# Latent attention of a hybrid layer: value products in pairs, scores a tile ahead, and a new pace for the row gathers

## The chip, the cores and the metric

One core of a Trainium2 chip runs the whole program in one launch. The metric is the device time of one execution in microseconds; a run's figure is that of the core.

Five engines work side by side, each on its own stream of instructions: TensorE (PE in the profile; its weight loads are PEld), VectorE (DVE), ScalarE (ACT), GpSimd (POOL) and SyncE (SP). Sixteen DMA engines move data between the chip's memory and the core. A scheduler sets the order of each engine's stream when the program is built; on the chip the streams keep that order and wait for each other through semaphores.

## The reference

One layer of a diffusion backbone over 256 context tokens and 1024 latent tokens of 1024 values. Each token passes modulation by a condition vector, a norm and one input projection, which feeds windowed attention and a recurrent mixer; their outputs go through one output projection; then each token looks up experts (PEER) in two tables of 16384 rows. Cut to the part that matters here:

```
def latent_attention(q, k, v, sink, *, cos, sin, k_ctx, v_ctx):      # 8 query heads, 2 key/value heads of 64
    ...
    s_band = jnp.einsum('bnqkgd,bnckd->bkgnqc', qb, k_band).astype(jnp.float32) * ATTN_SCALE   # 3 blocks of 128 keys
    s_ctx = jnp.einsum('bnqkgd,bckd->bkgnqc', qb, k_ctx).astype(jnp.float32) * ATTN_SCALE      # 256 context keys
    s_band = jnp.where(mask, s_band, -jnp.inf)                                                 # |q - k| <= 128
    p = jax.nn.softmax(jnp.concatenate([s_band, s_ctx, sk], axis=-1), axis=-1)                 # sk: the head's sink logit
    o = (jnp.einsum('bkgnqc,bnckd->bnqkgd', p_band, v_band)
         + jnp.einsum('bkgnqc,bckd->bnqkgd', p_ctx, v_ctx))

def peer(h, w_query, sub_keys, u_tab, v_tab):
    ...
        u = jnp.take(u_tab, eid, axis=0)                                # 8 heads x 16 rows of u a token
        act = jax.nn.gelu(jnp.einsum('td,thkd->thk', xb, u))
        vv = jnp.take(v_tab, eid, axis=0)                               # and of v
        return jnp.einsum('thk,thkd->td', (g * act).astype(vv.dtype), vv)
```

## The kernel before

**Stages.** The program runs modulation, projections, recurrence, attention, output projection and ranking for the context (to about 360 us), then projection and recurrence for the latent tokens (to 541), the latent attention (541 to 792), the output projection of the latent tokens (to 905), the ranking of experts (to about 1215), the lookups that turn the ranking into gates ("spread") with the experts' first groups ("early"; to about 1814), and the expert stage proper ("dense", to 3620). Its end is the last residuals and norms.

**Experts in two ways.** Six of the eight latent token tiles compute all 16384 experts densely on TensorE: `u` (a product of the tokens with the table's rows), a gelu, a product with the gates (`a*gt`, line 763), a split in a high and a low part (line 137) and a product with `v`, added up in `rot` (lines 743, 744) and `res`. Two context tiles and the other two latent tiles fetch their own rows instead: `mix` (line 827) issues for each of 4 tiles 128 row gathers of `u` and 128 of `v` on GpSimd (lines 838, 852), 512 KB each, and VectorE takes one product over 128x1024 for each (lines 841, 858). These 1024 gathers stand in a queue. `tick(us)` (line 112) takes as many from it as the given time holds steps: 1.9 us a step as a rule (`F_STEP`), 4.0 in "ret", 1.0 in "early", 2.2 in the expert stage (`D_STEP`). So `tick` is not a time on the chip; it places the gathers among the other instructions. What is left in the queue is issued at the end.

**Latent attention.** `attend` (line 387) handles one tile of 128 queries after another, and in it one of two head groups `g` (4 query heads that share one key head) after the other. Keys are split into a high part `kh` and a low part `kl` in a reduced float format: 8 copies on ScalarE (line 402) and 4 subtractions on VectorE (line 403) ahead of all scores. The tile's queries are split in the same way (lines 412, 413) and stacked, high on 64 rows and low on the other 64. For each head four score products go into two accumulators of one `s` tile: 256 context columns and up to 384 window columns, each once with the stacked queries on 128 rows against `kh` (line 431) and once with the 64 rows of the high queries against `kl` (line 432); two products with a mask close the head (line 435). VectorE takes the maximum (line 438) and the shift (439), ScalarE the exponential with its sum (440). After the four heads, their probabilities are divided by the sum: by the string NORM, two heads on ScalarE (448), one on GpSimd and one on VectorE (450). Then for each block `j` of 128 keys, 4 transposes (455), one copy by ScalarE to `pT` (457) and one product with the values, 64 columns of the array wide (462), accumulate into 64 of the 128 rows of `po`; ScalarE copies the result over the queries (463). A tile in the middle has 5 blocks, one at an end 4. Each group ends with `tick(13)`.

A few rows of memory are shared: `kh`, `kl` and the split queries lie in tiles that later hold the normed activations (`hha`, `hla`). `finish` (the output projection) opens its weight pool before the attention.

**What sets the order.** All of this is written in program order, with buffers rotating (`bufs`), and the scheduler moves instructions ahead within an engine where buffers allow it, as the order below shows for scores among value products.

## Time and profile before

| | us |
|---|---|
| median of 3 runs (lowest to highest) | 3672.97 (3672.86 to 3684.63) |
| the profiled execution | 3664.41 |
| its span | 3662.5 |
| busy: TensorE, VectorE | 3302.0, 3111.3 |
| busy: GpSimd, ScalarE | 1705.7, 1462.7 |
| mean granted TensorE clock | 0.957 of full |

The span runs from the first to the last instruction of one profiled execution; the execution's time is measured around it. A busy share over the whole span mixes stages that have different limits, so the rows below are read by stage. In a group, "idle before" is the time in which the engine stood still just before these instructions, and behind the arrow is what ended it. The end of a TensorE instruction is modelled, and its instructions overlap in the pipeline; how long it needs for one is read from the distance of starts.

### The profile page before, as it was taken

To read this page: it belongs to the slowest core of one execution; us is meant where nothing else is said; L and a number is where in the kernel's file an instruction comes from. 1 tells how busy PE (TensorE), PEld (TensorE's weight loads), DVE (VectorE), ACT (ScalarE), POOL (GpSimd) and SP (SyncE) were. 2 spreads that over 40 slices of the span, in tenths; PEclk is the share of its full clock that TensorE was granted. 3 is DMA by queue.
4 is the path that set the end of the run, shared out by engine and by line. 5 is a ranking of instruction groups with operands and counts; after the bars stand their busy time and mean duration, and the time that the engine had idled before them with its cause. 6 is when DMAs were issued, how large, how long until landed. Compare 5 with 4: busy or idle time off the path is not lost.

```text
span 3662.5 us, 48593 instructions
## 1 busy us (share of the span) xinstructions
PE 3302.0 (90%) x16982; PEld 2718.4 (74%) x16982; DVE 3111.3 (85%) x6710; ACT 1462.7 (40%) x2272; POOL 1705.7 (47%) x1162
## 2 busy tenths in 40 slices
PE   7888879888699978888699999999999999999995
PEld 4477644434598967777688888888888888888885
DVE  4549886767799999998678898899999999899988
ACT  5743645533312334433233333333434333333333
POOL 0012454556631233246435565566556655555652
PEclk9799988999899999999799999999999999999998
DMA  8342654468851257789878898899888899888884
GB/s 330 114 155 84 210 201 133 150 213 288 303 157 39 90 180 217 233 260 308 288 243 298 300 318 299 307 331 329 314 311 309 313 329 323 320 309 308 318 319 178
DMA packets 349143, 918.20 MB, mean 251 GB/s; under 512 B 29145, under 2 KB 150105, under 8 KB 345825
## 3 DMA queue, kind: packets, MB, share of 16 engines
q0 software_dynamic: 147456, 536.94, 42.6%
q1 hardware_dynamic: 201440, 378.16, 30.1%
q8 instruction: 133, 2.18, 0.2%
q14 instruction: 114, 0.93, 0.1%
HBM read 834.48 MB, written 80.50 MB: 250 GB/s over the span
## 4 chain that ended last, share of the span: by engine, by line
PE 39%; DVE 20%; DMA 7%; issue 4%; POOL 1%; ACT 1%; SPq 0%; POOLq 0%; DVEq 0%; ACTq 0%
PE u L142 6%; PE u L140 6%; PE u L141 6%; PE rot L140 4%; PE rot L142 4%; PE rot L141 4%; DMA a<-ad 3%; DVE row L841 3%; DVE acc L858 3%; PE res L140 3%; PE res L142 3%; PE res L141 3%; DMA ad<-a 2%; DVE acc L744 2%; DVE oh L678 1%
## 5 line engine op out<-in xcount | busy, mean ns | idle before, releaser
L838 POOL DMA_INDIRECT row<-in_peer_u,eid x512 | 713.1, 1393 | 646.4 <-DVE row L841 240.5
L852 POOL DMA_INDIRECT row<-in_peer_v,eid x512 | 702.7, 1372 | 636.4 <-DVE acc L858 354.8
L140 PE MATMUL u<-hh,uh 128*128 128x384 f32 x2048 | 705.1, 344 | 40.3 <-ACT a L1009 38.2
L142 PE MATMUL u<-hh,ul 128*128 128x384 f32 x2048 | 705.4, 345 | 12.0 <-POOL ul L137 12.0
L141 PE MATMUL u<-hl,uh 128*128 128x384 f32 x2048 | 703.8, 344 | 0.0
L858 DVE SCALAR_TENSOR_TENSOR acc<-row,w,acc 128x1024 f32<-128x1024 f32 x508 | 664.7, 1308 | 28.4 <-DMA row<-in_peer_v,eid 27.1
L841 DVE SCALAR_TENSOR_TENSOR row<-row,h 128x1024 f32<-128x1024 f32 x512 | 631.1, 1246 | 60.1 <-DMA row<-in_peer_u,eid 60.0
L743 ACT ACTIVATE q<-rot 128x512 f32<-128x512 f32 x504 | 300.1, 596 | 495.1 <-PE rot L142 296.0
L140 PE MATMUL rot<-vh,ah 128*128 128x512 f32 x1024 | 408.4, 399 | 23.1 <-ACT q L743 22.5
L140 PEld LDWEIGHTS u<-hh,uh 128*128 128x128 f32 x2048 | 392.1, 191 | 48.4 <-ACT a L1009 42.0
L142 PEld LDWEIGHTS u<-hh,ul 128*128 128x128 f32 x2048 | 392.3, 192 | 15.5 <-POOL ul L137 12.9
L141 PE MATMUL rot<-vl,ah 128*128 128x512 f32 x1024 | 400.9, 392 | 0.0
L142 PE MATMUL rot<-vh,al 128*128 128x512 f32 x1024 | 400.4, 392 | 0.0
L141 PEld LDWEIGHTS u<-hl,uh 128*128 128x128 f32 x2048 | 392.5, 192 | 5.7 <-issue 2.0
L744 DVE TENSOR_TENSOR acc<-q,acc 128x512 f32<-128x512 f32 x504 | 340.7, 686 | 60.6 <-ACT q L743 57.6
L140 PE MATMUL mm<-hh,wh 128*128 128x256 f32 (+2 forms) x848 | 287.5, 339 | 11.8 <-ACT wh L136 11.8
L142 PE MATMUL mm<-hh,wl 128*128 128x256 f32 (+2 forms) x848 | 289.5, 342 | 6.2 <-POOL wl L137 3.6
L141 PE MATMUL mm<-hl,wh 128*128 128x256 f32 (+2 forms) x848 | 284.8, 336 | 0.0
L136 ACT ACTIVATE uh<-u 128x1024 fp32r<-128x1024 f32 x128 | 135.8, 1061 | 359.9 <-PE u L141 295.7
L140 PEld LDWEIGHTS rot<-vh,ah 128*128 128x128 f32 x1024 | 193.5, 189 | 82.7 <-ACT q L743 43.9
L137 POOL TENSOR_TENSOR ul<-u,uh 128x1024 fp32r<-128x1024 f32 x44 | 132.0, 2999 | 231.5 <-ACT uh L136 214.7
L142 PEld LDWEIGHTS rot<-vh,al 128*128 128x128 f32 x1024 | 193.3, 189 | 41.4
(266 smaller groups left out, 6030.8 us busy)
## 6 DMA issues: line engine op xcount, KB each, us to landing
u<-in_ut SPq DMA_DIRECT2D x128, 512.0 KB
v<-in_peer_v SPq DMA_DIRECT2D x128, 512.0 KB
gd<-stg SPq DMA_DIRECT2D x12, 4096.0 KB
gt<-gd SPq DMA_DIRECT2D x64, 768.0 KB
w<-in_w_mod SPq DMA_DIRECT2D x24, 1024.0 KB
ad<-a SPq DMA_DIRECT2D x88, 192.0 KB
a<-ad SPq DMA_DIRECT2D x44, 384.0 KB
w<-in_w_query SPq DMA_DIRECT2D x32, 512.0 KB
```

Source lines behind the costliest of these rows:

```text
L136: A.activation(hi, src, AF.Copy)
L137: return (eng or V).tensor_tensor(lo, src, hi, op=OP.subtract)
L140: T.matmul(out, lhs[0], rhs[0], start=first, stop=False)
L141: T.matmul(out, lhs[0], rhs[1], start=False, stop=False)
L142: T.matmul(out, lhs[1], rhs[0], start=False, stop=last)
L678: V.tensor_tensor(oh.rearrange(four, j=2), o2.rearrange(four, j=2), pairs(gh, ts), op=OP.mult)
L743: A.activation(q, p, AF.Copy)
L744: tick(share / (2 * (N_DENSE - N_RES)), V.tensor_tensor(y, q, y, op=OP.add))
L838: G.indirect_dma_start(out=u, out_offset=None, in_=i["peer_u"], in_offset=bass.IndirectOffsetOnAxis(ap=eid[:, k:k + 1], axis=0))
L841: V.scalar_tensor_tensor(u, u, 1.0, h2, op0=OP.mult, op1=OP.mult, accum_out=act[:, j:j + 1])
L852: G.indirect_dma_start(out=v, out_offset=None, in_=i["peer_v"], in_offset=bass.IndirectOffsetOnAxis(ap=eid[:, k:k + 1], axis=0))
L858: V.scalar_tensor_tensor(acc, v, w[:, j:j + 1], acc, op0=OP.mult, op1=OP.add)
```

## The change

1. Keys: both parts are now 128 rows high, the low part copied to the other 64 rows too, so that the score products with `kl` take the same stacked queries as those with `kh`. The keys are split in four pieces (context, columns 0 to 256, 256 to 512, 512 to 1024): 24 copies and 8 subtractions. All of them still stand before the first score product in the order.
2. Values: `scores(t, g)` of a tile come before `values` of the tile before it. For each block, both head groups' transposes and copies are followed by two products that use the two halves of the array's columns, one issued right behind the other, into the two halves of one `po`. There are 38 such pairs; ScalarE evicts 128x512 once for a tile (8) in place of 64x512 twice (16). Buffers: `pr` 4 instead of 2, `pT` 4 instead of 3.
3. Normalisation of the latent heads: all on VectorE (64 instructions; before 16 on VectorE, 16 on GpSimd, 32 on ScalarE).
4. Gathers: `tick(0.6)` for each head and `tick(1.3)` for each block replace `tick(13)` for each group, 88 us of steps instead of 208; `D_STEP` is 2.05 instead of 2.2. The count stays 1024.
5. Pools: the attention has its own key tiles, `hha` and `hla` are made after it, and the weights of `finish` lie on the other side of the memory. Its first loads keep their place in SyncE's order.

```
@@ -51,15 +51,13 @@
-D_STEP = 2.2
+D_STEP = 2.05
...
-NORM = "AAGV"
@@ -384,84 +382,109 @@
-    def attend(cond, st, ps, tiles, qT, kT, vv, spare=None):
+    def attend(cond, st, ps, tiles, qT, kT, vv):
...
-            for src, ks in ((kc, slice(0, base)), (kT, slice(base, base + S))):
+            kh, kl = (st.tile([P, 2, S + base], F32R, name=f"k{n}") for n in "hl")
+            for src, b0, k0, k1 in ((kc, 0, 0, base), (kT, base, 0, 256), (kT, base, 256, 512), (kT, base, 512, S)):
+                ks, cols = slice(b0 + k0, b0 + k1), slice(k0, k1)
                 for g in range(2):
-                    for r in range(2):
-                        A.activation(kh[half[r], g, ks], src[half[g]], AF.Copy)
-                    V.tensor_tensor(kl[half[g], ks], src[half[g]], kh[half[g], g, ks], op=OP.subtract)
-        for t in tiles:
+                    A.activation(kh[half[g], g, ks], src[half[g], cols], AF.Copy)
+                    V.tensor_tensor(kl[half[g], g, ks], src[half[g], cols], kh[half[g], g, ks], op=OP.subtract)
+                    A.activation(kh[half[1 - g], g, ks], src[half[g], cols], AF.Copy)
+                    A.activation(kl[half[1 - g], g, ks], kl[half[g], g, ks].bitcast(F32), AF.Copy)
+
+        qsp = {}
+
+        def scores(t, g):
...
+            if lat and g == 0:
+                qs = qsp[t] = st.tile([P, 2, 4, P], F32R, name="qs", bufs=2)
...
+            pr = st.tile([P, 4, W], F32, name="pr", bufs=4)
...
-                            T.matmul(out, qs[gs, g, c], kl[gs, k:k + w], start=False, stop=(bank == 0), skip_group_check=True)
+                        T.matmul(out, qh, kl[:, g, k:k + w], start=False, stop=(bank == 0), skip_group_check=True)
...
+                tick(0.6)
...
+            for c in range(4):
+                if lat:
+                    V.tensor_scalar(pr[:, c], pr[:, c], den[:, c:c + 1], None, op0=OP.mult)
+                else:
+                    A.activation(pr[:, c], pr[:, c], AF.Copy, scale=den[:, c:c + 1])
+            return pr
...
-                    T.matmul(po[gs], vb, pT, start=(j == 0), stop=(j == nk - 1))
-                A.activation(qT[gs, :, ts], po[gs], AF.Copy)
-                tick(13)
+        def values(t, prs, js):
...
+            for j in range(nk)[js]:
+                if j == 0:
+                    outs[t] = ps.tile([P, 4, P], F32, name="po")
+                po = outs[t]
+                pTs = []
+                for pr in prs:
                     pt = ps.tile([P, 4, P], F32, name="pt")
                     for c in range(4):
                         T.transpose(pt[:, c], pr[:, c, j * P:(j + 1) * P], ident)
-                    pT = st.tile([P, 4, P], F32, name="pT", bufs=3)
+                    pT = st.tile([P, 4, P], F32, name="pT", bufs=4)
                     A.activation(pT, pt, AF.Copy)
...
+                vb = vc[:, j] if lat and j < 2 else vv[:, lo + j - (2 if lat else 0)]
+                ins = T.matmul(po[half[1]], vb[:, half[1]], pTs[1], start=(j == 0), stop=(j == nk - 1))
+                with tc.issue_after(ins.ins):
+                    T.matmul(po[half[0]], vb[:, half[0]], pTs[0], start=(j == 0), stop=(j == nk - 1))
+                tick(1.3)
+                if j == nk - 1:
+                    A.activation(qT[:, :, ts], po, AF.Copy)
+
+        ahead = None
+        for t in tiles:
+            now = []
+            for g in range(2):
+                now.append(scores(t, g))
+                if ahead:
+                    values(*ahead, slice(g * 3, g * 3 + 3))
+            ahead = t, now
+        values(*ahead, slice(0, None))
@@ -930,58 +951,56 @@
...
-                attend(1, pool(es, "lat"), pool(es, "lps", space=PSUM), range(N_LAT), qT, kT, vv, (hha, hla))
...
+        fin = finish(fs, 1, range(N_LAT), qT, gy, lambda t: dest(t))
+        next(fin)
+        next(fin)
+        phase("lattend")
+        with ExitStack() as es:
+            attend(1, pool(es, "lat"), pool(es, "lps", space=PSUM), range(N_LAT), qT, kT, vv)
+        side[0] = "right"
+        hx = pool(ctx, "hx")
```

TensorE in the middle of the latent attention before (`s`: scores, `po`: values' accumulator, `pt`: transposed probabilities, `hh`, `hl` hold keys and queries):

```order
L462 MATMUL po<-pT,vv 64x512
L455 MATMUL pt<-ident,pr 128x128 x4
L462 MATMUL po<-pT,vv 64x512
L455 MATMUL pt<-ident,pr 128x128 x4
L431 MATMUL s<-hh,hl 128x256
L432 MATMUL s<-hl 128x256
L431 MATMUL s<-hh,hl 128x384
L432 MATMUL s<-hl 128x384
```

The same place now (`kh`, `kl`: keys, `qs`: queries; lines 431 and 432 are the scores, 467 the transposes, 472 and 474 the products with the values):

```order
L472 MATMUL po<-pT,vv 64x512
L474 MATMUL po<-pT,vv 64x512
L467 MATMUL pt<-ident,pr 128x128 x8
L431 MATMUL s<-kh,qs 128x256
L432 MATMUL s<-kl,qs 128x256
L431 MATMUL s<-kh,qs 128x384
L432 MATMUL s<-kl,qs 128x384
L472 MATMUL po<-pT,vv 64x512
L474 MATMUL po<-pT,vv 64x512
```

A value product stood alone, with four transposes behind it; now two stand together, eight transposes stand in a row, and scores of the next tile lie between a block's transposes and its products.

GpSimd shortly before the expert stage, before (`ul` is the low part of the experts' `u`, lines 852 and 838 are row gathers, `eid` the row numbers of one token tile):

```order
L838 DMA row<-in_peer_u,eid_2301 128x1024 x5
L137 TENSOR_TENSOR ul<-u,uh 128x1024
L838 DMA row<-in_peer_u,eid_2301 128x1024 x8
L137 TENSOR_TENSOR ul<-u,uh 128x1024
L852 DMA row<-in_peer_v,eid_2301 128x1024 x5
L137 TENSOR_TENSOR ul<-u,uh 128x1024
L852 DMA row<-in_peer_v,eid_2301 128x1024 x5
L137 TENSOR_TENSOR ul<-u,uh 128x1024
L852 DMA row<-in_peer_v,eid_2301 128x1024
```

And now (line 135 is the split, 873 and 859 the gathers):

```order
L135 TENSOR_TENSOR ul<-u,uh 128x1024
L873 DMA row<-in_peer_v,eid_2156 128x1024
L135 TENSOR_TENSOR ul<-u,uh 128x1024
L873 DMA row<-in_peer_v,eid_2156 128x1024
L135 TENSOR_TENSOR ul<-u,uh 128x1024
L873 DMA row_16254<-in_peer_v,eid_2156 128x1024
L873 DMA row_16266<-in_peer_v,eid_2156 128x1024
L873 DMA row_16515<-in_peer_v,eid_2156 128x1024
L135 TENSOR_TENSOR ul<-u,uh 128x1024 x6
L859 DMA row<-in_peer_u,eid_2297 128x1024 x3
```

Between the last splits ahead of the expert stage stood groups of gathers; now the last six splits follow each other, and the gathers come in the expert stage.

VectorE at the end of the program before, from the last additions on (`acc_16445` to `acc_16448` are the dense tiles' sums, line 858 the products of gathered rows, 816 and 817 the residuals):

```order
L744 TENSOR_TENSOR acc_16445<-q,acc_16445 128x512
L858 SCALAR_TENSOR_TENSOR acc<-row_31868,w,acc 128x1024
L744 TENSOR_TENSOR acc_16445<-q,acc_16445 128x512
L816 TENSOR_TENSOR acc<-acc,row_31873 128x1024
L744 TENSOR_TENSOR acc_16446<-q,acc_16446 128x512
L817 TENSOR_TENSOR h_31609<-acc,h_31609 128x1024
L744 TENSOR_TENSOR acc_16446<-q,acc_16446 128x512
L744 TENSOR_TENSOR acc_16447<-q,acc_16447 128x512
L147 TENSOR_SCALAR rs_m<-ss 128x1
```

And now (line 765 is the addition, 879 the product of a gathered row, 837 and 838 the residuals):

```order
L765 TENSOR_TENSOR acc_16237<-q,acc_16237 128x512
L879 SCALAR_TENSOR_TENSOR acc<-row_31893,w,acc 128x1024
L765 TENSOR_TENSOR acc_16238<-q,acc_16238 128x512
L879 SCALAR_TENSOR_TENSOR acc<-row,w,acc 128x1024
L765 TENSOR_TENSOR acc_16238<-q,acc_16238 128x512
L879 SCALAR_TENSOR_TENSOR acc<-row,w,acc 128x1024
L837 TENSOR_TENSOR row<-row,vh 128x1024
L879 SCALAR_TENSOR_TENSOR acc<-row,w,acc 128x1024
L838 TENSOR_TENSOR gt<-row,gt 128x1024
L879 SCALAR_TENSOR_TENSOR acc<-row,w,acc 128x1024
L837 TENSOR_TENSOR row<-row,vh 128x1024
L879 SCALAR_TENSOR_TENSOR acc<-row_31948,w,acc 128x1024
```

Products of gathered rows, which ended among the first additions, now stand behind all of them and among the first residuals.

## Rows read from the trace of the kernel before

**Rows 1.** By stretch: start:end, its length, busy time and instructions of each engine, PEclk, DMA, GB/s.

```profile
541.00:566.00 25.00, 22.54 (x55) 12.89 (x56) 16.58 (x33) 13.81 (x29) 5.42 (x4) 0.50 0.43 150
596.00:626.00 30.00, 27.66 (x110) 12.88 (x109) 21.14 (x40) 18.96 (x39) 15.40 (x10) 1.00 0.45 146
1215.00:1500.00 285.00, 246.18 (x1828) 223.72 (x1827) 282.59 (x1027) 119.02 (x156) 95.58 (x42) 0.97 0.59 184
1500.00:1814.00 314.00, 246.98 (x1801) 224.61 (x1799) 261.95 (x560) 111.46 (x139) 141.96 (x84) 0.91 0.84 270
1812.00:3620.00 1808.00, 1775.45 (x8613) 1563.30 (x8614) 1619.14 (x2067) 693.96 (x1045) 1009.36 (x707) 0.99 0.87 309
```

**Rows 2.** Timeline of TensorE, latent attention: start, time, line, operation, tiles, form, count.

```profile
634.55 0.66 PE L455 MATMUL pt<-ident,pr 128*128 128x128 f32 x4
634.96 0.36 PE L431 MATMUL s<-hh,hl 128*128 128x256 f32 x1
635.25 0.38 PE L432 MATMUL s<-hl 64*128 64x256 f32 x1
635.56 0.44 PE L431 MATMUL s<-hh,hl 128*128 128x384 f32 x1
635.93 0.44 PE L432 MATMUL s<-hl 64*128 64x384 f32 x1
636.31 0.28 PE L435 MATMUL s<-maskb,identb 128*128 128x128 bf16 x2
636.40 0.36 PE L431 MATMUL s<-hh,hl 128*128 128x256 f32 x1
...
637.75 1.07 PE L462 MATMUL po<-pT,vc 128*64 128x512 f32 x2
638.75 0.66 PE L455 MATMUL pt<-ident,pr 128*128 128x128 f32 x4
```

**Rows 3.** Timeline of TensorE, input projection of the context.

```profile
70.13 0.28 PE L141 MATMUL mm<-hl,wh 128*128 128x256 f32 x1
70.25 0.28 PE L142 MATMUL mm<-hh,wl 128*128 128x256 f32 x1
```

**Rows 4.** Timeline of TensorE, experts' first product.

```profile
1230.88 0.34 PE L140 MATMUL u<-hh,uh 128*128 128x384 f32 x1
1231.05 0.34 PE L141 MATMUL u<-hl,uh 128*128 128x384 f32 x1
```

**Rows 5.** Timeline of TensorE, modulation; a row gathers eight passes.

```profile
14.06 1.94 PE L192 MATMUL p<-w,sig 128*32 128x512 f32 x8 [2.77 <-DMA w<-in_w_mod]
```

**Rows 6.** Groups of TensorE, 541 to 793: count, busy, mean ns, idle before, releasers.

```profile
L462 PE MATMUL po<-pT,vv 128*64 128x512 f32 x88 | 47.2, 618 | 20.6 <-ACT pT L457 19.2 <-issue 1.3
L431 PE MATMUL s<-hh,hl 128*128 128x256 f32 x80 | 33.5, 418 | 19.4 <-DVE hl L413 15.9 <-ACT pr L440 3.5
```

**Rows 7.** Groups of VectorE, 541 to 793.

```profile
L858 DVE SCALAR_TENSOR_TENSOR acc<-row,w,acc 128x1024 f32<-128x1024 f32 x41 | 52.8, 1288 | 4.2 <-DMA row<-in_peer_v,eid 3.7
L438 DVE TENSOR_REDUCE den<-s 128x1 f32<-128x640 f32 x48 | 39.5, 823 | 48.4 <-PE s L435 46.9 <-PE pt L455 1.4
L439 DVE TENSOR_SCALAR negm<-den,nsink 128x1 f32<-128x1 f32 x64 | 12.3, 205 | 0.1
L413 DVE TENSOR_TENSOR hl<-qT,hl 64x512 fp32r<-64x512 f32 x16 | 11.0, 686 | 1.4 <-ACT hl L412 0.9
L450 DVE TENSOR_SCALAR pr<-pr,den 128x640 f32<-128x640 f32 x12 | 10.7, 888 | 0.0
```

**Rows 8.** Timeline of VectorE, latent attention.

```profile
643.77 0.55 DVE L450 TENSOR_SCALAR pr<-pr,den 128x640 f32<-128x640 f32 x1
```

**Rows 9.** Chain of waits, 1700 to 1760: start, length, what.

```profile
1722.96 9.00 DMA row<-in_peer_u,eid
```

**Rows 10.** Timeline of VectorE, end of the program.

```profile
3617.58 0.69 DVE L744 TENSOR_TENSOR acc<-q,acc 128x512 f32<-128x512 f32 x1 [1.44 <-ACT q L743]
```

**Rows 11.** Timeline of TensorE, first value product of the latent attention.

```profile
565.69 1.97 PE L462 MATMUL po<-pT,vc 128*64 128x512 f32 x2
```

More of the change, by code (lines that the diff above doesn't have):

```diff
@@ L478, in weights @@
                 nc.sync.dma_start(w[:, k], i["w_out"][k, :, c0:c0 + HW])
-        def start():
-            weights(0)
-            return mod_row(wp.tile([P, D], F32, name="ga1"), cond, 0)
-        ga1 = start()
+        yield
+        weights(0)
+        ga1 = mod_row(wp.tile([P, D], F32, name="ga1"), cond, 0)
         yield
@@ new lines, in body, with after @@
+        kv = pool(fs, "lkv")
+        kT = kv.tile([P, S_LAT], F32, name="kT")
+        vv = kv.tile([P, N_LAT, P], F32, name="vv")
+        phase("lproj")
+        with ExitStack() as es:
+            work = []
+            def after(m):
+                if m < 4:
+                    if m == 0:
+                        work.append(pool(es, "lro"))
+                        rotate(work[2], work[1], kT)
+                    rotate(work[2], work[1], qT[:, m])
+                if m >= 10:
+                    if not work:
+                        work.append(pool(es, "lst"))
+                        work.append(pool(es, "lgs", space=PSUM))
+                    phase("lrecur")
+                    recur(1, *work, gy, qT, [m - 10])
+                    phase("lproj")
+            project(es, 1, qT, gy, kT, vv, qT, after)
@@ new lines, in body @@
+        side[0] = "right"
+        gat = pool(ctx, "gat")
+        queue.extend(mix(t) for t in range(N_CTX))
+        side[0] = "left"
+        fin = finish(fs, 1, range(N_LAT), qT, gy, lambda t: dest(t))
+        next(fin)
+        next(fin)
+        phase("lattend")
+        with ExitStack() as es:
+            attend(1, pool(es, "lat"), pool(es, "lps", space=PSUM), range(N_LAT), qT, kT, vv)
+        side[0] = "right"
+        hx = pool(ctx, "hx")
+        hha = hx.tile([P, KD, TD], F32R, name="hh")
@@ L979, in body, with dest @@
+        hla = hx.tile([P, KD, TD], F32R, name="hl")
+        hs = ctx.enter_context(ExitStack())
+        hx = pool(hs, "hxb")
+        TG = S_LAT - TD
+        hhb = hx.tile([P, KD, TG], F32R, name="hh")
+        hlb = hx.tile([P, KD, TG], F32R, name="hl")
+        def dest(t):
+            hh, hl, u = (hha, hla, t) if t < N_DENSE else (hhb, hlb, t - N_DENSE)
+            return hh, hl, slice(u * P, (u + 1) * P)
+        side[0] = "left"
         phase("fin")
-        side[0] = "right"
         for _ in fin:
@@ L982, in body @@
             pass
-        fs2.close()
-        side[0] = "left"
     phase("ret")
```

131 lines of the change are left out of this document (37 added, 94 removed).

## The prediction

> **What bounds the kernel now.** I read the profile from coarse to fine: busy time by stage, then the stage that the change rewrites by instruction group and by single instruction, then the stages that receive the gathers it gives away. In the table by stage [rows 1] each stage has its own limit. In the latent attention (541 to 792) TensorE is busy 27.66 of 30 us at full clock while VectorE has 21.14 and the transfers 0.45: TensorE sets the pace. From 1215 to 1500 VectorE is busy 282.59 of 285. From 1500 to 1814 the transfers stand at 0.84, and no engine is full. In the expert stage (1812 to 3620) TensorE has 1775 of 1808 us, VectorE 1619, transfers 0.87 at 309 GB/s: TensorE bound, with both others near. So time comes out of the attention only by relieving TensorE, and a gather (one 512 KB row transfer and one VectorE product) costs something different in each stage it is moved to.
>
> **Scores.** In single instructions [rows 2] one head steps 634.96, 635.25, 635.56, 635.93, 636.31, and its two masks end at 636.40: 1.44 us. Its 64-row products alternate with 128-row ones, and each step is 0.29 to 0.31 us for 256 columns and 0.37 for 384. Where neighbours are all 128 rows high, 256 columns step by 0.12 [rows 3] and 384 by 0.17 [rows 4]. The change makes the low-part products 128 rows high with the same stationary operand, so a head becomes 2 x 0.12 + 2 x 0.17 + 0.09 = 0.67 us; I take 0.72, as heads still meet 64-column products now and then. Bounds: 1.44 (nothing gained) and 0.67. 64 heads, most of them of this size, save 0.72 us each: 46 us of TensorE time.
>
> **Values.** 76 products (10 in a middle tile, 8 at each end) now become 38 pairs. One product with its two passes holds the engine from 637.75 to 638.75, 1.00 us, with four transposes 0.41 behind it [rows 2]. Products in different column strips stand together in one place only, the stage at 14 us: eight passes of 512 columns, that is four products in four strips, are through in 1.94 us [rows 5]. One after another, at 1.00 each, they would take 4; side by side each costs 0.49, so two cost no less than 0.97 and no less than the 1.00 of one. So a pair lies between 1.00 (side by side) and 2.00 (one after the other); I take 1.0, by that row. Gain: 76 - 38 = 38 us, at worst 0. The waits for the copied transposes, 19.2 us [rows 6], mostly go, because the next scores now lie between transposes and products. The Trainium skill speaks against the whole gain: "TensorE: Matmul & The Clock Gate" (Part 3, What overlaps and what doesn't) says that matmuls start and end strictly in program order. If the two passes of one half had to be through before the other half's second, a pair would be three steps, about 1.5 us by rows 2, and 19 us of the gain would be lost on TensorE; the row at 14 us goes against it, and in the sum it changes little since VectorE is next.
>
> **What is late next.** A middle tile asks of TensorE 8 x 0.72 + 10 x 0.41 + 5 x 1.0 = 15 us, against 29 before (250 us, less 16 of start, over 8 tiles). Of VectorE it asks [rows 7]: 8 maxima x 0.823, 8 x 0.205, 2 subtractions x 0.686, about 1 us of small ones, eight normalisations instead of two, and gathers. A normalisation averages 0.888, but stands at 0.55 where GpSimd does not run its own [rows 8]; GpSimd's are gone, so 8 x 0.55 = 4.4 (7.1 at the other bound). Gathers between the first and last attention instruction on VectorE: 63 before, 29 after, so 3.6 a tile x 1.26 = 4.5. Sum 19.5 us (22.2): VectorE becomes the bound. The stage is 8 x 19.5 = 156, plus the start (TensorE's wait of 15.9 us before the first scores [rows 6] stays, since all key pieces are still split ahead of them), plus about 9 for the last tile's values (10 x 0.41 + 5 x 1.0), which have no scores beside them. That is 181, so **-70 us**. Bounds: -90 (end tiles are smaller) and -35 (22.2 a tile, and 1.5 us of waits for scores in each). ScalarE loses its normalisations and half its evictions and is under both. The other pools and the extra yield I cost at nothing: the output weights keep their place on the load queue, and the attention covers them; without that cover one transfer, some 9 us as in rows 9.
>
> **Gathers elsewhere.** The program's order has the same 1024, moved. Against before, the count is 6 higher from the end of the attention to the end of the ranking (all of it ahead of the output projection's VectorE work, where TensorE bounds, so at nothing; 6 x 1.25 = 8 if that cover were gone), 9 lower in the lookups, 26 lower from there to the first gate product, 53 higher in the expert stage and 10 higher behind its last gate product. VectorE is full during the lookups [rows 1], so 9 x 1.25 = **-11**. Where the transfers stand at 0.84, 26 gathers are 26 x 0.524 MB = 13.6 MB, 44 us at the 309 GB/s of the expert stage, at the most; the chain there shows single gathers of 9.00 us on it [rows 9], but also other transfers which keep their size. Between 0 and -44 I take **-20**.
>
> In the expert stage 53 x 1.25 = 66 us more VectorE work meets 1808 - 1619 = 189 us of idle time [rows 1]: 0 if all of it falls into gaps, 66 if none does. TensorE has 33 us idle and decides; VectorE keeps 123 us of slack, so I am near the low end: **+20**. The ten behind the last gate product have no such gaps: VectorE waits there once for 1.44 us [rows 10] and then works nearly without a pause to the end. 10 x 1.2 = 12, less that wait: **+10** (5 to 15).
>
> **Sum.** The profiled execution took 3664.4 us (span 3662.5): 3664.4 - 70 - 11 - 20 + 20 + 10 = 3593. The median of the runs is 8.6 above that execution: 3602, forecast **3600**.
>
> **Rivals.**
> (1) *The gathers are paid in full in the expert stage.* VectorE at 1685 of 1808 us stands in its own fixed waits (for the copies of ScalarE, for the gate transfers), and TensorE with it. Then +66 instead of +20: 3648. For it: VectorE's idle time is a tenth of the stage, spread thin. Against: TensorE hardly waits today.
> (2) *The pairs do not run side by side*, so this part of the change does not do what it says: a pair is 2.00, TensorE needs 20 us a tile, as much as VectorE, and the two collide. I give 22 to 23 a tile, attention -45: 3627. For it: no 128x64 pair in this trace. Against: rows 5.
> (3) *Transfers bound the expert stage.* 53 x 0.524 = 27.8 MB at 309 GB/s are 90 us: 3664.4 - 70 - 31 + 90 + 10, 3672 on the median's scale, no change. Against: a busy share of 0.87 leaves room, and TensorE, not a transfer, is what is full there.
> (4) *Slower: TensorE's clock falls in the attention.* Around its wait of 15.9 us before the first scores it ran at a granted 0.50 (the 1.2 GHz level), to 566 [rows 1]; two passes of a value product last 1.97 there instead of 1.07 [rows 2, 11]. If the many short waits for VectorE keep it there, a tile's 15 us become 30, the stage 16 + 8 x 30 + 18 (the last values at that level) = 274 instead of 250: 3664.4 + 24 - 31 + 20 + 10, on the median's scale 3696. It decides from a granted clock of about 0.6 (15/0.6 = 25 a tile); above it VectorE still bounds. Against: from 596 on it stands at 1.00, though TensorE waits for copies all along. A page of the Trainium skill has this rival: "TensorE: Matmul & The Clock Gate" (A second HAM failure mode: psum-queue depth-cycling) says that frequent micro-idles between groups of matmuls can make the clock swing between its levels. The trace does not agree so far: the waits for copies, 19.2 us in all, did not lower it.
>
> **How the numbers follow.** Forecast 0.60 (alone 3560 to 3640), rival 1 0.16, rival 2 0.10, rival 3 0.06, rival 4 0.08. The terms' ends give 3664.4 - 90 - 11 - 44 + 0 + 5 = 3524 and 3664.4 - 35 - 11 - 0 + 66 + 15 = 3699; both need all terms at one end. Cutting 1 in 10 at either side leaves 3548 to 3665. What a measurement can tell from no change is 0.5%, 18 us, so faster means under 3655: nearly all of the forecast and of rival 2, two thirds of rival 1, together 0.80. The same: rival 3 and the rest of rival 1, 0.12. Slower: rival 4, 0.08.
>
> **What would show it.** Scores: steps of 0.12 and 0.17 and a head of 0.7. Pairs: four passes in about 1.0 us, transposes following; two of them or three times 0.48 would be rival 2. Attention: some 180 us long, VectorE above 90%, TensorE waiting for VectorE, clock 1.0. Normalisations at 0.55. Expert stage: about 20 us longer between its first and last gate product, TensorE idle up from 33 to some 50. Last gate product to end: 62 instead of 52. I am wrong if the attention stays above 215 us, or if the expert stage grows by more than 50.

## The result, and the profile after

The changed kernel takes 3566.74 us (median of 4 runs, 3561.74 to 3570.26) against 3672.91 for the kernel before beside it: ratio 0.972, 95% interval 0.9687 to 0.9754, 106 us. Its profiled execution took 3568.34 us, 96 less than that of the kernel before. Read between the same instructions of both traces, these 96 us are:

| stretch | before | after | difference | forecast |
|---|---|---|---|---|
| start to the last product of the latent projection | 524.3 | 511.0 | -13.3 | 0 |
| to the first latent score | 18.1 | 22.9 | +4.8 | in -70 |
| latent attention, to the first product of the output projection | 249.5 | 172.0 | -77.5 | -70 |
| output projection and ranking, to the first lookup | 512.7 | 516.6 | +3.9 | 0 |
| lookups | 410.0 | 394.6 | -15.4 | -11 |
| to the first gate product | 99.9 | 93.3 | -6.6 | -20 |
| expert stage, to the last gate product | 1796.1 | 1795.7 | -0.4 | +20 |
| end, to the last residual on VectorE | 47.3 | 56.3 | +9.0 | +10 |

The spans end 4.6 and 4.1 us behind the last row, so the forecast's "62 instead of 52" for the end, counted to there, came out as 60.4 instead of 51.8.

The stages of the profile after, in the columns of [rows 1]: the beginning of the latent attention, its middle, 285 us ahead of the early groups, the expert stage:

```profile
534.00:546.00 12.00, 8.99 (x39) 7.96 (x39) 10.14 (x22) 8.11 (x17) 1.45 (x2) 0.50 0.15 48
576.00:606.00 30.00, 26.78 (x170) 16.32 (x170) 28.12 (x62) 22.30 (x50) 6.22 (x6) 1.00 0.35 101
1133.00:1418.00 285.00, 249.24 (x1840) 227.11 (x1839) 276.36 (x1090) 123.08 (x160) 75.15 (x33) 0.95 0.55 165
1710.00:3506.00 1796.00, 1767.69 (x8579) 1559.94 (x8580) 1674.05 (x2151) 687.55 (x1040) 1126.43 (x762) 0.99 0.90 326
```

In the middle of the attention VectorE stands at 28.12 of 30 us where it had 21.14, and TensorE at 26.78. In the third row, which answers to 1215 to 1500 before, VectorE is busy 276 of 285 us. In the expert stage VectorE has risen from 1619 us in 1808 to 1674 in 1796, and the transfers from 0.87 to 0.90; the stage is no longer than before.

TensorE in the latent attention after, one pair and one head (columns as in [rows 2]):

```profile
605.60 0.64 PE L472 MATMUL po<-pT,vv 128*64 128x512 f32 x1 [0.38 <-ACT pT L469]
605.61 0.64 PE L474 MATMUL po<-pT,vv 128*64 128x512 f32 x1
606.08 0.59 PE L472 MATMUL po<-pT,vv 128*64 128x512 f32 x1
606.09 0.59 PE L474 MATMUL po<-pT,vv 128*64 128x512 f32 x1
606.61 0.66 PE L467 MATMUL pt<-ident,pr 128*128 128x128 f32 x4
608.01 0.66 PE L467 MATMUL pt<-ident,pr 128*128 128x128 f32 x4 [0.75 <-ACT pT L469]
609.36 0.64 PE L472 MATMUL po<-pT,vv 128*64 128x512 f32 x1 [0.69 <-ACT pT L469]
...
612.22 0.29 PE L434 MATMUL s<-maskb,identb 128*128 128x128 bf16 x2
612.32 0.36 PE L431 MATMUL s<-kh,qs 128*128 128x256 f32 x1
612.52 0.28 PE L432 MATMUL s<-kl,qs 128*128 128x256 f32 x1
612.64 0.34 PE L431 MATMUL s<-kh,qs 128*128 128x384 f32 x1
612.81 0.34 PE L432 MATMUL s<-kl,qs 128*128 128x384 f32 x1
612.99 0.60 PE L467 MATMUL pt<-ident,pr 128*128 128x128 f32 x4
```

The two halves of a pair start 10 ns apart or less, their second passes 0.48 later, and the transposes follow 1.01 us after the first start: one pair costs what one product cost. A head's four products step by 0.20, 0.12, 0.17 and 0.18, 0.67 instead of 1.35 without its masks; with 0.10 for the masks it is 0.77 instead of 1.44. Rows 605.60 to 609.36 are one whole block without scores in between: the pair holds TensorE for 1.01 us, the first transposes and their copy take 1.40, the second ones and theirs 1.35, and the next pair starts 3.76 us after the last. In these, TensorE stands still for 0.75 and 0.69 us, since there is one `pt` tile: the second transposes wait until ScalarE has copied the first. What TensorE waits for from the start of the attention on (us in total, times, longest):

```profile
PE s L431 <- DVE qs L414: 20.7, 1, 20.7
PE pt L467 <- ACT pT L469: 13.3, 20, 0.7
PE po L472 <- ACT pT L469: 12.3, 21, 0.7
PE s L431 <- ACT pr L439: 4.3, 6, 2.3
PE pt L467 <- DVE pr L448: 0.3, 1, 0.3
```

The 20.7 us are the start, ahead of the first score. Behind it TensorE waits 0.3 us for VectorE, but still 25.6 us, 41 times, for ScalarE's copies of transposes; before it was 21.5, of which [rows 6] has the 19.2 of the window's blocks. From the first score to the output projection TensorE is busy 140.6 us of the 172.0, VectorE 150.3. VectorE's normalisations stand at 0.56, where [rows 8] has 0.55, and its maxima wait 7.7 us instead of the 48.4 of [rows 7]:

```profile
L437 DVE TENSOR_REDUCE den<-s 128x1 f32<-128x640 f32 x48 | 38.8, 818 | 7.7 <-PE s L434 6.2 <-PE po L474 1.1
L448 DVE TENSOR_SCALAR pr<-pr,den 128x640 f32<-128x640 f32 x48 | 23.9, 560 | 0.0
```

### The profile page after: what moved, and what is told of

Read it like the earlier page. It is cut to its first block, busy times and chain, and to the rows that moved or that the text cites. A ratio compares the mean times of both kernels' runs of the same rounds, so it can differ in the third digit from the quotient of the medians.

```text
span 3566.5 us, 48580 instructions
## 1 busy us (share of the span) xinstructions
PE 3210.4 (90%) x16982; PEld 2704.1 (76%) x16982; DVE 3111.0 (87%) x6762; ACT 1429.9 (40%) x2242; POOL 1716.4 (48%) x1146
## 4 chain that ended last, share of the span: by engine, by line
PE 43%; DVE 22%; issue 8%; DMA 8%; POOL 3%; ACT 2%; SPq 0%; POOLq 0%; DVEq 0%; ACTq 0%
PE u L138 6%; PE u L140 6%; PE u L139 6%; PE rot L138 5%; PE rot L140 5%; PE rot L139 5%; DVE acc L879 3%; DVE row L862 3%; DMA row<-in_peer_u,eid 2%; PE res L138 2%; PE res L139 2%; PE res L140 2%; DMA row<-in_peer_v,eid 2%; DMA ad<-a 2%; DVE oh L699 1%
## 5 line engine op out<-in xcount | busy, mean ns | idle before, releaser
L859 POOL DMA_INDIRECT row<-in_peer_u,eid x512 | 749.9, 1465 | 603.3 <-DVE acc L879 201.7
L873 POOL DMA_INDIRECT row<-in_peer_v,eid x512 | 719.9, 1406 | 583.6 <-DVE acc L879 283.7
L138 PE MATMUL u<-hh,uh 128*128 128x384 f32 x2048 | 707.1, 345 | 22.4 <-ACT a L1028 22.4
L862 DVE SCALAR_TENSOR_TENSOR row<-row,h 128x1024 f32<-128x1024 f32 x512 | 623.0, 1232 | 62.8 <-DMA row<-in_peer_u,eid 62.6
L139 PEld LDWEIGHTS u<-hl,uh 128*128 128x128 f32 x2048 | 394.6, 193 | 4.5
L135 POOL TENSOR_TENSOR ul<-u,uh 128x1024 fp32r<-128x1024 f32 x44 | 122.8, 2791 | 277.8 <-ACT uh L134 237.5
```

The costliest lines, as they stand in the source:

```text
L135: return (eng or V).tensor_tensor(lo, src, hi, op=OP.subtract)
L138: T.matmul(out, lhs[0], rhs[0], start=first, stop=False)
L139: T.matmul(out, lhs[0], rhs[1], start=False, stop=False)
L859: G.indirect_dma_start(out=u, out_offset=None, in_=i["peer_u"], in_offset=bass.IndirectOffsetOnAxis(ap=eid[:, k:k + 1], axis=0))
L862: V.scalar_tensor_tensor(u, u, 1.0, h2, op0=OP.mult, op1=OP.mult, accum_out=act[:, j:j + 1])
L873: G.indirect_dma_start(out=v, out_offset=None, in_=i["peer_v"], in_offset=bass.IndirectOffsetOnAxis(ap=eid[:, k:k + 1], axis=0))
```

## The experiments

"Attention" is the time from the first latent score to the first product of the output projection, read in each trace; the kernel before has 249.5 and the changed one 172.0. The 95% interval stands behind each ratio to the kernel before.

| run | median us | ratio | attention us |
|---|---|---|---|
| e1_low64 | 3622.34 | 0.9891 (0.9846 to 0.9935) | 232.7 |
| e2_alone | 3607.54 | 0.9836 (0.9797 to 0.9874) | 210.5 |
| e3_norm | 3578.08 | 0.9764 (0.9725 to 0.9803) | 183.5 |
| e4_ctx | 3565.24 | 0.9721 (0.969 to 0.9753) | 171.5 |
| e5_pt3 | 3574.84 | 0.9742 (0.9711 to 0.9773) | 194.6 |
| e6_att63 | 3636.30 | 0.9905 (0.9871 to 0.9939) | 197.1 |
| e7_gath | 3629.64 | 0.9908 (0.9882 to 0.9934) | 259.2 |
| e8_d200 | 3576.90 | 0.9758 (0.973 to 0.9786) | 171.1 |
| e9_nokl | 3567.54 | 0.9714 (0.9681 to 0.9747) | 175.3 |
| e10_hold | 3632.22 | 0.9891 (0.9858 to 0.9925) | 177.5 |
| e11_lazy | 3574.23 | 0.9733 (0.9708 to 0.9758) | 175.3 |
| e12_both | 3625.23 | 0.9907 (0.9875 to 0.994) | 169.7 |

How well a stage repeats is seen from e8_d200, which has the changed kernel's instructions up to the expert stage: its attention is 171.1, its output projection 153.8 (155.2), its lookups 394.6. Ahead of the attention it is 3.5 us shorter, in the early groups (from the lookups to the first gate product) 3.0 longer: differences of this size mean nothing.

### Parts of the attention undone

**e1_low64**, low keys on 64 rows:

```diff
-T.matmul(out, qh, kl[:, g, k:k + w], ...)
+T.matmul(out, qsp[t][gs, g, c], kl[gs, g, k:k + w], ...)
```

> The changed kernel with one part undone: the products with the low keys use 64 rows and the 64 rows of the high queries again (the other rows of kl stay unused; with that the product of both low parts, which the change added, is left out as in the kernel before). Theory (VectorE paces the new attention at some 20 us a tile, TensorE needs some 16): a head costs about 1.4 instead of 0.7 us on TensorE, 43 us over 64 heads, TensorE comes to 21 or 22 a tile, so about 10 to 25 us of it shows: 3577 to 3592. Rival 1 (TensorE still paces it): all 43 us, 3610. Rival 2 (the full-height keys are worth nothing here): 3567.

Measured 3622.34; the attention takes 61 us more, above even the rival that has TensorE pace it. The steps are those of the kernel before (0.29 to 0.31 and 0.37), 43 us in all; for the rest, about 18 us, there is the clock (columns as above):

```profile
546.00:576.00 30.00, 28.52 (x77) 15.51 (x78) 17.58 (x43) 10.48 (x25) 1.88 (x2) 0.50 0.12 35
576.00:606.00 30.00, 27.92 (x116) 14.47 (x112) 18.04 (x40) 15.71 (x35) 2.82 (x3) 0.81 0.18 53
696.00:726.00 30.00, 27.52 (x106) 14.75 (x106) 18.92 (x46) 14.42 (x35) 6.38 (x6) 0.79 0.40 122
```

The granted clock stays at 0.50 (its 1.2 GHz level) up to 576, stands at 0.81 in the next 30 us and falls again late, to 0.79 here and 0.64 from 726 to 756, where the changed kernel has 0.89 in the first of these stretches and 1.00 from 576 to 705. Rival 4's low clock is there, but not its reason, many short waits: TensorE is busy 28.52 of the first 30 us. The 64-row products alone don't explain it either, since the kernel before has the same ones and stood at 1.00 from 596 on [rows 1].

**e2_alone**, value products one at a time:

```diff
-ins = T.matmul(po[half[1]], vb[:, half[1]], pTs[1], ...)
-with tc.issue_after(ins.ins):
-    T.matmul(po[half[0]], vb[:, half[0]], pTs[0], ...)
+T.matmul(po[half[r]], vb[:, half[r]], pT, ...)      # behind each copy, in the loop over prs
```

> The changed kernel with the pairs undone: each value product is issued behind its own copy of the transposes, without the link that puts two together; scores still run a tile ahead, and one po tile holds both halves. Theory (VectorE paces): 38 us more on TensorE (76 products of 1.0 us instead of 38 pairs of 1.0), TensorE at 20 to 21 us a tile, so 0 to 20 us of it shows: 3567 to 3587. Rival (TensorE paces): 38 us, 3605. In both, the two passes of a product stand 0.48 us apart and alone.

Measured 3607.54, the attention 38.5 us longer: the whole price of 38 products on TensorE, as the rival says. TensorE's waits for copies stayed:

```profile
PE po L473 <- ACT pT L469: 26.9, 43, 0.7
```

and VectorE's maxima waited for scores, 35.0 us instead of 8.1:

```profile
DVE den L437 <- PE s L434: 35.0, 27, 3.6
```

**e3_norm**, normalisation spread:

```diff
-if lat:
-    V.tensor_scalar(pr[:, c], ...)
+if lat and "AAGV"[c] != "A":
+    {"V": V, "G": G}["AAGV"[c]].tensor_scalar(pr[:, c], ...)
```

> The changed kernel with the normalisation of the latent heads spread again: two of four on ScalarE, one on GpSimd, one on VectorE. Theory (VectorE paces): VectorE is relieved of 48 x 0.56 = 27 us there; the scheduler puts 18 more gathers in front of the attention's last maximum, which give back 18 x 1.25 = 22 of it, and the lookups behind have 26 gathers less; so attention about the same and the lookups up to 26 x 1.25 = 33 us shorter: 3535 to 3567. Rival (the normalisation on one quick engine is what shortened each tile's chain): ScalarE's 0.82 and GpSimd's 2.1 us come back into the chain, attention 15 to 30 us longer: 3580 to 3600.

Measured 3578.08, whose interval overlaps that of the changed kernel. The attention became 11.5 us longer, with 18 more gathers in it, and the lookups 16.5 shorter. Less VectorE work for the normalisation did not shorten the attention; since the gathers moved with it, it doesn't tell more.

### Who paces the attention

**e9_nokl**, TensorE relieved, and **e10_hold**, VectorE relieved:

```diff
 # e9_nokl
-T.matmul(out, qh, kl[:, g, k:k + w], start=False, stop=(bank == 0), ...)
 # e10_hold
-tick(0.6) ... tick(1.3)
+if t == n - 1 and g == 1 and c == 3: behind.append(ins.ins)   # gathers only after the last normalisation
+tick(87.8)                                                    # after the attention
```

> The changed kernel without the score products with the low keys (two of the four products of a head; this part of the computation is left out): TensorE has 128 instructions less in the latent attention, 80 x 0.12 + 48 x 0.17 = 18 us, VectorE and ScalarE have what they had. In the profile after, TensorE waits for VectorE 0.3 us there in all, and 26 us for copies of ScalarE, while VectorE is 93% busy. Theory (TensorE's work and its waits for copies pace the latent attention): the stage is 18 us shorter, 154 instead of 172, total 3549. Rival (VectorE paces it, as forecast): the stage stays within 5 us of 172, total 3562 to 3567. Between the two (both are full by now): some 9 us.

> The changed kernel with all row gathers held back until the latent attention's last normalisation (the 48 that ran ahead of it in the latent projection too), and then taken at the pace of the output projection; from the first gate product on it is the same. To be read by stage. VectorE has 29 gathers or 36 us less in the latent attention. Theory (TensorE paces it): the stage stays at 165 to 172 us. Rival (VectorE paces it): 136 to 145 us. The projection before it tells what its 48 gathers cost: nothing if TensorE bounds there. The output projection and the lookups behind have to take 77 more: at 1.25 us each up to 96, at nothing in gaps of the output projection's VectorE some 30; total 3580 to 3640.

Neither shortened the stage: 175.3 and 177.5, so the theory of e9_nokl (154) and the rival of e10_hold (136 to 145) both fell. In e9_nokl TensorE's waits for copies and score tiles rose from 29.9 to 40.7 us:

```profile
PE po L471 <- ACT pT L468: 18.4, 23, 1.4
PE pt L466 <- ACT pT L468: 14.0, 21, 1.0
PE s L431 <- ACT pr L438: 8.3, 8, 3.2
```

and the granted clock is 0.60 in its first 32 us and 0.80 in its last 42, where the changed kernel has 0.71 and 1.00: a part of what was saved went there. In e10_hold VectorE's relief turned into waits for scores, 43.7 us instead of 8.1:

```profile
DVE den L437 <- PE s L434: 43.7, 26, 6.5
```

The granted clock was 0.51 in its first 30 us, against 0.69 after. By e10_hold VectorE was not what paced the attention: that is the theory's side. By e9_nokl the scores' work taken from TensorE does not come back as time, which the theory missed. The held gathers were dear elsewhere: the output projection and the ranking took 44.8 us more for 37 more gathers, 1.2 each, and the total is 65 us above that of the changed kernel.

**e12_both**, both reliefs in one kernel (the two edits above):

> The two reliefs of the latent attention together: the products with the low keys left out (18 us less of TensorE; this part of the computation is left out) and the row gathers held back behind the latent attention (36 us less of VectorE). Each alone left the stage, from its first score to the output projection, where it was: 175 and 177 us against 172. Theory (TensorE with its waits for copies and VectorE meet at the same length, so that one relief alone shows nothing): with both, the stage falls to 152 to 162 us. Rival (a chain through all engines, from the scores by maximum, exponential, normalisation, transposes and copies, sets the length, whatever the engines' work): 168 to 177 us again. The total is that of the held gathers, less what the stage gives: 3610 or 3632.

169.7, in the range of the rival, and the theory that two equal bounds meet fell. TensorE's waits for ScalarE are now 41.9 us:

```profile
PE pt L468 <- ACT pT L470: 18.3, 31, 0.7
PE po L473 <- ACT pT L470: 12.6, 19, 0.7
PE s L431 <- ACT pr L438: 11.0, 18, 2.8
```

The clock can be kept out of this by looking at the third to the seventh tile alone, in which it was granted in full in all of these runs. "Five tiles" runs on VectorE from the first maximum of the third tile to that of the eighth, with the busy time of both engines in it; "block" is the shortest distance from one pair of value products to the next in the whole attention:

| run | five tiles | TensorE busy | VectorE busy | block |
|---|---|---|---|---|
| changed kernel | 92.4 | 80.4 | 85.5 | 3.75 |
| e9_nokl | 92.7 | 72.8 | 84.9 | 3.76 |
| e10_hold | 93.3 | 80.8 | 64.1 | 3.76 |
| e12_both | 94.1 | 73.8 | 65.8 | 3.75 |
| e2_alone | 118.0 | 105.3 | 87.3 | 4.81 |

With 8 us less of TensorE's work, with 21 us less of VectorE's, and with both, the five tiles take the same 92 to 94 us. The eight us between e12_both and e10_hold lie in the first two tiles, where the clock differs. What stays is the loop of a block as in the rows above: transposes, copy, transposes, copy, pair. In no run of the first four does it take less than 3.75 us, and on average it takes 4.0 (37 distances in 148.8 us in the changed kernel). Where one product more stands in it, in e2_alone, it takes 1.05 us more, and the five tiles 25.6 more for their 23 pairs. So, with as few gathers as here, the loop and not an engine's work sets the length of these tiles.

**e5_pt3**, more tiles for the transposes, to take the waits for copies away:

```diff
-s = ps.tile(..., name="s", bufs=3 if lat else 2)
+s = ps.tile(..., name="s", bufs=2)
-pt = ps.tile([P, 4, P], F32, name="pt")
+pt = ps.tile([P, 4, P], F32, name="pt", bufs=3 if lat else 1)
```

> The changed kernel with the accumulators given out otherwise: three pt tiles for transposes (one before) and two s tiles (three before). Undoing the pairs cost the attention its full 38 us, so TensorE with its waits of 0.7 us for copies (41 of them, 26 us) may set the pace and not VectorE. Theory (TensorE's work plus these waits paces): the waits for a free pt mostly go, 13 us, and nothing takes their place; the order also puts 28 more gathers before the attention's last maximum and as many fewer into the lookups, so the attention is shorter by 0 to 13 us and the lookups by 10 to 30: 3530 to 3557. Rival (VectorE paces): the 28 gathers lengthen the attention by 28 x 1.25 = 35 us, and the lookups give about that back: 3560 to 3580.

The waits for copies went (25.6 to 1.4 us), others came: for score tiles, of which there are fewer, and for VectorE, which got 24 more gathers before the last value product:

```profile
PE s L431 <- ACT pr L439: 23.1, 15, 3.4
PE pt L467 <- DVE pr L448: 20.2, 9, 6.5
PE po L472 <- ACT pT L469: 1.4, 4, 0.7
```

The attention is 22.6 us longer, the lookups 17.9 shorter, and the total lies in the rival's range. The loop is broken, for two pairs now come as close as 0.91 us, but as a test of what that is worth the run is spoilt by those gathers: VectorE is busy 178 us of the 194. The granted clock, 0.83 over the attention where the changed kernel has 0.95, is a second reason that the run cannot tell apart.

### Gathers

**e7_gath**, only the pace, on the kernel before, and **e6_att63**, the old pace on the changed kernel:

```diff
 # e7_gath
-tick(13)
+tick(5.5)
-D_STEP = 2.2
+D_STEP = 2.05
 # e6_att63
-tick(0.6) ... tick(1.3) ... D_STEP = 2.05
+tick(1.416) ... tick(3.068) ... D_STEP = 2.2
```

> The kernel before with only the gathers paced otherwise: tick(5.5) for tick(13) and a step of 2.05 us in the expert stage; the attention's instructions are the old ones. The order has as many gathers as before up to the start of the lookups, 36 fewer within them, 26 fewer from there to the first gate product, 53 more in the expert stage, 10 more behind its last gate product. Theory: attention unchanged, expert stage unchanged, lookups and early groups 22 to 45 us shorter, tail 9 longer: 3637 to 3660. Rival (moving gathers brings nothing by itself): 3673 to 3682.

> The changed kernel with the gathers paced as before: ticks in the attention 2.36 times as long and a step of 2.2 us in the expert stage; the order then has 21 more gathers before the attention's last maximum, 30 more before the end of the lookups, 63 more before the first gate product, 10 fewer behind the last one. Theory (the fewer gathers save in lookups and early groups, as forecast, and cost nothing in the expert stage): expert stage as long as now, tail 9 shorter, lookups to the first gate product about 22 longer; attention 0 to 10 longer if TensorE paces it, 26 if VectorE does: 3580 to 3590, or 3606. Rival (the expert stage does pay for the 53 gathers it took over, and something else made up for it): expert stage 20 or more shorter, 3560.

e7_gath gains 35 us by its medians: lookups 45.1 us shorter for 36 gathers (1.25 each), early groups 5.1, end 8.4 longer, expert stage +0.8 with 53 more gathers. Its attention is 9.7 longer with no more gathers: the granted clock fell to 0.66 from 673 to 703 us, in a stretch in which TensorE was busy 27.3 of 30, and the tile there took 39.0 us where its neighbours took 30 to 33. e6_att63 came out 30 us above the theory's upper value. Its expert stage is 2.7 shorter and its end 9.2, as expected, but lookups and early groups are 19.8 and 22.4 longer (22 expected for both), the output projection and the ranking 13.1 for 9 more gathers, and the attention 25.1 for 20 more, 1.25 each. The lookups grew with no more gathers in them (39 products in both traces), so other things move them too. In the attention TensorE now waits for VectorE's normalisations, 13.8 us instead of 0.3, and the granted clock is 0.78 from 660 on:

```profile
PE pt L467 <- DVE pr L448: 13.8, 3, 12.2
```

So neither half of the change is worth more than 1% alone, and together they are worth 2.8%: the new attention has room for few gathers, and the old one, with VectorE at 21.14 of 30 us [rows 1], had room for its own.

**e8_d200**, the expert stage asked to take all:

```diff
-D_STEP = 2.05
+D_STEP = 2.0
```

> The changed kernel with a step of 2.0 us in the expert stage in place of 2.05: all gathers then lie before its last gate product, 14 more in the stage and none behind. Theory (a gather is free in the expert stage and costs its 1.2 us at the end): tail shorter by 9 to 12 us, expert stage unchanged: 3556. Rival (VectorE's slack in the expert stage is used up by now): the stage grows by 14 x 1.25 = 17 us, 3567 to 3575.

The end fell by 8.9 us as expected, but the expert stage grew by 21.1 for 14 gathers, and VectorE's idle time in it did not shrink (124 us, 122 after). TensorE's waits in it, 36.1 us after,

```profile
PE rot L138 <- ACT q L764: 16.1, 9, 5.0
PE res L138 <- ACT ah L134: 14.9, 3, 10.5
PE u L140 <- DVE ul L135: 4.7, 1, 4.7
```

are 51.7 here:

```profile
PE res L138 <- ACT ah L134: 21.1, 8, 10.3
PE rot L138 <- ACT q L764: 19.5, 18, 5.4
PE res L140 <- DVE al L135: 6.2, 2, 3.7
PE u L140 <- DVE ul L135: 4.9, 1, 4.9
```

### Two starts

**e4_ctx**, the old order for the context's attention, and **e11_lazy**, key pieces split where they are first needed:

```diff
 # e4_ctx
-attend(0, st, ps, range(N_CTX), qT, kT, vv)
+attend_ctx(0, st, ps, range(N_CTX), qT, kT, vv)     # the loop of the kernel before
 # e11_lazy
-for src, b0, k0, k1 in ((kc, 0, 0, base), (kT, base, 0, 256), (kT, base, 256, 512), (kT, base, 512, S)):
+# ahead of scores(t, 0): pieces 1 and 2 for t = 0, piece 3 for t = 1, piece 4 for t = 3
```

> The changed kernel with the old order (one head group after the other, one value product at a time) for the context's attention alone; the latent attention is unchanged. Theory: the changed function also serves the context, whose attention (125 to 190 us) became some 10 us shorter by pairs and scores ahead, which the prediction left out: 3577 with the whole difference by 195 us. Rival (what is gained before the latent attention comes from pools and the order of loads, not from the context's attention): 3567.

> The changed kernel with the key pieces split where they are first needed: the context's and columns 0 to 256 before tile 0, 256 to 512 before tile 1, 512 to 1024 before tile 3. The profile after has TensorE wait 20.7 us before the first scores, since all four pieces and the queries are split ahead of them. Theory (that wait is the split's length, and ScalarE has room later, 22 of 30 us busy): the wait falls to about 11 us, the stage behind grows by 0 to 3, total 3558. Rival (ScalarE's copies for the later pieces come between its copies of transposes, for which TensorE waits): what the start gains the tiles lose, 3567.

In e4_ctx the first latent score starts at 542.6, 8.7 us later than after and where the kernel before had it: the context's attention did gain by the change. Its last value product stands at 182.3 us in the kernel before and in e4_ctx, at 172.1 in the changed kernel. But the output projection took 145.2 us instead of 155.2 and gave it back. TensorE waits less for the normed tokens there, in the changed kernel and in e4_ctx:

```profile
L248 PE MATMUL tr<-ident,x 128*128 128x128 f32 x56 | 11.2, 364 | 28.3 <-ACT x L537 28.3
```

```profile
L248 PE MATMUL tr<-ident,x 128*128 128x128 f32 x56 | 9.6, 325 | 21.9 <-ACT x L573 21.9
```

Why the same instructions wait 28.3 us in one and 21.9 in the other stays open. In e11_lazy the start wait fell from 20.7 to 14.3 us, but the attention grew by 3.3, the output projection by 6 and the lookups by 10: no gain.

## Why the prediction was right, and where it was not

The forecast was 3600 us and 73 us of gain; measured were 3566.74 and 106, inside the range. Direction and place are right: three quarters of the gain lie in the latent attention.

**Scores and values** came nearly as worked out: 0.77 a head with its masks (0.72 taken), 1.01 a pair (1.0 taken). e1_low64 and e2_alone show that both are needed, each worth at least what its TensorE time says. Rival 2 is out, and so is rival 4 for the changed kernel: the clock is granted in full from 576 to 705. (The forecast's ground against it, full clock from 596 on, was not quite so: 656 to 686 before has 0.94.) The two halves' passes alternate: first of one, first of the other, then both second ones. What the Trainium skill states of program order ("TensorE: Matmul & The Clock Gate", Part 3, What overlaps and what doesn't) agrees with that as far as starts tell it (the first half starts ahead of the second, 605.60 and 605.61), and at this order it costs nothing. The row at 14 us [rows 5], which the forecast read as 0.49 a product, says less: the trace's clock records begin at 23.5 us only. From 24.07 on, the passes of all four strips start within 20 ns and the next four 0.45 us later, so four products run in the time of one there; the 1.0 for a pair doesn't change by it.

**The step that failed is "what is late next".** It said that "VectorE becomes the bound", and "Values" that the waits for the copied transposes "mostly go". The waits rose from 21.5 to 25.6 us, and VectorE relieved by 36 us gave nothing (e10_hold). In place of VectorE stands the loop of a block through the one `pt` tile: the forecast priced a block at 2 x 0.41 + 1.0 = 1.82 us of TensorE's work and put its two copies at nothing, and the loop takes 3.76 at the least. VectorE's own sum, 19.5 a tile, was a little high too: it worked 17.1 a tile in the five tiles. The stage is 22.2 us to the first pair, 148.8 to the last and 1.0 behind it: 172.0. Scores and gathers mostly find room beside that, up to the point at which VectorE is full (e6_att63).

That the forecast's -70 met the measured -72.7 (-77.5 and +4.8 in the table) is luck, by a slip in the sum. Its 181 holds the wait at the start; the 250 that it was taken from does not, for that wait ends at 542.35 with the first score, where the 249.5 begin. Like for like the forecast had 165 behind the first score, 85 less than before, with an unchanged start.

**Left out: the function also serves the context.** 13.3 us were gained before the latent attention, 9.1 of them by e4_ctx in the context's attention (8.7 at the first latent score). In the total of e4_ctx nothing is seen of it.

**Gathers.** The lookups' term came near (-15.4 for the forecast -11), and the end's (+9.0 for +10). Its price of 1.25 a gather is e7_gath's; in e3_norm and e5_pt3, whose lookups have 26 and 27 gathers fewer than the changed kernel's, they are only 16.5 and 17.9 shorter, 0.65 each. The early groups gave 6.6 instead of 20: with the gathers gone, TensorE's wait for the gelu's output there falls from

```profile
PE u L140 <- ACT a L1009: 27.3, 3, 21.6
```

to

```profile
PE u L138 <- ACT a L1028: 8.5, 1, 8.5
```

but TensorE's work fills 76 of the 93 us that are left, a bound that the forecast did not look for. The order also moved 89 of its products with `u` into this stretch (421, before 332), 62 of them out of the lookups, which shortens those and lengthens this. And the expert stage, +20 in the sum, took its 53 gathers for nothing, the lower bound. They went into VectorE's gaps, as the idle column says, before

```profile
L763 DVE TENSOR_TENSOR a<-a,gt 128x768 f32<-128x768 f32 x128 | 122.0, 953 | 35.4 <-DMA a<-ad 30.7 <-ACT a L762 3.8 <-issue 0.3
L137 DVE TENSOR_TENSOR ul<-u,uh 128x1024 fp32r<-128x1024 f32 x84 | 102.4, 1221 | 73.5 <-ACT uh L136 69.1 <-issue 4.4
```

and after:

```profile
L784 DVE TENSOR_TENSOR a<-a,gt 128x768 f32<-128x768 f32 x127 | 121.0, 953 | 8.9 <-DMA a<-ad 7.4 <-ACT a L783 1.3
L135 DVE TENSOR_TENSOR ul<-u,uh 128x1024 fp32r<-128x1024 f32 x84 | 101.9, 1220 | 36.9 <-ACT uh L134 30.5 <-PE rot L140 6.3
```

together 108.9 before and 45.8 after. Rivals 1 and 3 are out at this load; what e8_d200 shows 14 gathers further on fits rival 1. At the end the gathers stand among the residuals and nothing hides them:

```profile
3526.07 1.28 DVE L879 SCALAR_TENSOR_TENSOR acc<-row,w,acc 128x1024 f32<-128x1024 f32 x1
3534.72 1.21 DVE L838 TENSOR_TENSOR gt<-row,gt 128x1024 f32<-128x1024 f32 x1
3535.85 1.27 DVE L879 SCALAR_TENSOR_TENSOR acc<-row,w,acc 128x1024 f32<-128x1024 f32 x1
```

The profiled executions differ by 96 us where the terms gave 71; the 25 are the expert stage (+20) and the context (+13), less the early groups (-13), and the small ones.

## What to carry to other kernels

Give a job that can be placed anywhere a price in each stage: here one gather cost about 0.2 us in the latent projection (9 us for 43, e10_hold against after), 1.25 in the new attention, 1.2 in the output projection and the ranking, 0.65 to 1.25 in the lookups, 0.15 to 0.7 in the early groups (36 more in e10_hold, 33 in e6_att63), nothing in the expert stage up to a point and 1.5 beyond it, 0.9 at the end. Before calling the second busiest engine the next bound, price the loop that goes out to another engine and back through a single buffer: here it was twice the work that stands in it, and neither engine's relief shortened it. When two lengths are subtracted, see that both hold the same waits. And look for every caller of a function that is rewritten.

## What was not expected of the hardware

Two fp32 products in the two column halves of the array run their passes alternately, 10 ns apart or less, in the time of one (1.01 us, 1.00 for one alone before). And the granted clock does not follow TensorE's busy time: in e1_low64 it was 0.50 in a stretch in which TensorE was busy 28.5 of 30 us (546 to 576), after has 0.89 there at 26.1 us busy. What decides it stays open: the 64-row products of e1_low64 are also those of the kernel before, which had 1.00 from 596 to 626, and e10_hold, without them, had 0.51 in its first 30 us.
